# Attention in a two-layer backbone: queries split once and placed by transfers, the result norm taken for two heads at a time

## The chip, the cores and the metric

The kernel runs on one core of one Trainium2 chip. The metric is the device time of one execution in microseconds (us); of several runs the median is taken. Engines are named as the profile names them: PE is TensorE (PEld its weight loads), DVE is VectorE, ACT is ScalarE, POOL is GpSimd, SP is SyncE, which issues the kernel's transfers.

## The reference

The model has two layers over 512 latent tokens and 256 context tokens of width 1024. In each layer a norm is followed by one input projection whose columns feed three head groups: a gated MLP over positions, a differential attention, and a convolution module. An output projection joins them, and a gated FFN follows. The change touches the attention alone. It has 4 heads with two softmax maps each, queries and keys of 64 columns per map, values of 128:

```python
def diff_attn(q, k, v, lam):
    s = jnp.einsum("bqhmd,bkhmd->bhmqk", q.astype(F32), k.astype(F32)) * (B_QK_DIM ** -0.5)
    p = jax.nn.softmax(s, axis=-1)
    a = p[:, :, 0] - lam * p[:, :, 1]
    return jnp.einsum("bhqk,bkhd->bqhd", a, v.astype(F32))
...
yb = (rms_norm(o, P["subln_g"]) * (1.0 - lam_init)).astype(pa.dtype).reshape(b, n, B_WIDTH)
```

Context queries see the 256 context keys, latent queries all 768 keys. In layer 1 only latent tokens have queries. Everything is in float32.

## The kernel before

**Layout.** A product in float32 is made from rounded halves: each operand is split into a high part (type fp32r) and the remainder, and three products of the parts are added (`mm3`, lines 225 to 228). The attention products with the values, the transposes and the norms' sums are plain fp32 matmuls, which TensorE runs as two instructions each.

**Work items.** The attention stage is lines 712 to 868, once per layer. A work item n is a head h with 256 queries p: 12 items in layer 0 (first the 4 heads with context queries, which have 2 key tiles of 128, then 8 with latent queries and 6 key tiles), 8 in layer 1. Each is cut into two units of 128 queries. The loop at line 843 goes over the units: at unit u it prepares the next item's query (`q_prep`), computes the unit's two score maps, their maxima (DVE), exponentials with sums (ACT) and their difference (`scores`, `combine`); it transposes a unit two units later (`transp`), multiplies an item by its values three units later (`attn_v`), and normalizes its result five units later (`subln`).

**The query.** `q_prep` (lines 731 to 755) transposes a query into PSUM, 64 partitions for either map. The keys hold high and low parts on the two halves of the partitions, so the high part of the query of each map must stand on both halves: from the second item on one copy by ACT to `qn` and then two copies by ACT and two by POOL into `qh` place it. The low part is subtracted by DVE, 64 partitions at a time, into two standing buffers `qlz` whose other half was set to zero ahead (lines 718 to 724). Three buffers of `qh` let queries be prepared ahead of their scores; in both layers the first three are transposed at the start of the stage.

**The result norm.** The norm needs the sum of squares of 128 values plus a term with the epsilon that depends on the softmax sums (`dg`, a diagonal matrix that POOL makes per unit, line 788). `attn_v` copies the result and squares it on ACT, POOL adds `dg` (line 821), and `subln` sums over partitions by a matmul with a matrix of ones (line 828), takes logarithm and exponential on ACT, the product on DVE, and splits the result into `yBh` and `yBl`, which the output projection reads.

**Order.** Each engine runs its instructions in one fixed order. A planner sets it before the run from priorities (the order of the program, with shifts such as `SCP`) and its own estimates of durations. Beside the attention, output matmuls over the other two head groups (`wout` with part 0, lines 862 to 867) are issued into the stage as fill, on one PSUM buffer; their weights are loaded by SP and split by ACT and POOL. All transfers of the kernel are issued by SP. The launch reserves a space for descriptors of transfers issued by POOL (line 1092):

```python
_BACC = {"dynamic_dma_scratch_size": 256}
```

Of the kernel before, what the change touches and what calls it, by code (L numbers as in the profile page):

```python
# [9 lines left out]
F32 = mybir.dt.float32  # L10
F32R = mybir.dt.float32r
# [5 lines left out]
P = 128  # L17
# [9 lines left out]
QKD = 64  # L27
# [20 lines left out]
FB, WB, EB, QB = 1, 3, 5, 3  # L48
# [28 lines left out]
def tile_backbone(  # L77
# [6 lines left out]
    nc = tc.nc  # L84
    V, S, G, T = nc.vector, nc.scalar, nc.gpsimd, nc.tensor
# [19 lines left out]
    def sub_lo(o, a, hi, eng=None):  # L105
        (eng or V).tensor_sub(o, a, hi.bitcast(F32))  # L106
# [16 lines left out]
    ones = pers.tile([P, P], F32, name="ones")  # L123
# [158 lines left out]
    for l in range(DEPTH):  # L282
# [26 lines left out]
        with ExitStack() as ph:  # L309
            sac = ExitStack()  # L310
            sp = pool(sac, f"s1_{l}", side)
            ps = psum_pool(ph, f"ps1_{l}")
# [119 lines left out]
            for k2 in range(KD // 2):  # L432
                wh, wl = wsplit(wsrc(COL_C, k2), [2, 512], wengine(COL_C, k2), raw=pre.get(k2))
                for a in range(2):
                    k = 2 * k2 + a
                    for s in range(nseg)[::-1]:
                        t0, t1 = SEG[s]
                        for m in range(4):
                            ms = slice(m * P, (m + 1) * P)
                            o = pc[s][m][:, :t1 - t0]  # L440
# [3 lines left out]
                                     stop=k == KD - 1 and (s == 0 or m % 2 == 1))  # L444
# [5 lines left out]
            for s in range(nseg):  # L450
                n = SEG[s][1] - SEG[s][0]
# [19 lines left out]
            v = sp.tile([P, NT, AW], F32, name="v")  # L471
# [62 lines left out]
            sp = pool(ph, f"s1b_{l}", side)  # L534
# [47 lines left out]
            for t in range(NT_KV):  # L582
                x = kx.get(t)
                if x is None:
                    x = sp.tile([P, 512], F32, tag="kx", name="kx", bufs=KXB)
# [58 lines left out]
            for j in range(1, CONV):  # L644
                for c in range(2):
                    with low(CLOW[l]):
                        V.scalar_tensor_tensor(  # L647
                            out=cacc[:, c, :cn], in0=cin[:, c, j:j + cn], scalar=cw[:, l, c, j:j + 1],
# [5 lines left out]
            for x in range(2 * nseg):  # L654
                y = CH[l][0] + CH[l][1] * x
# [30 lines left out]
        yBh = yp.tile([P, 4, toks], F32R, name="yBh")  # L686
        yBl = yp.tile([P, 4, toks], F32R, name="yBl")
# [24 lines left out]
        with ExitStack() as ph:  # L712
            sp = pool(ph, f"s2_{l}", side)
            ps = psum_pool(ph, f"ps2_{l}")
            gsub = sp.tile([P, 1], F32, name="gsub")
            V.tensor_scalar_mul(gsub, sublt[:, l:l + 1], 1.0 - lam0)

            qlz = [sp.tile([P, 2, 256], F32R, name=f"qlz{x}") for x in range(2)]
            zero = sp.tile([P, 256], F32, name="zero")
            G.memset(zero, 0.0)  # L720
            for x in qlz:
                for m in range(2):
                    ms = slice((1 - m) * QKD, (2 - m) * QKD)
                    G.tensor_copy(x[ms, m], zero[ms])
            pairs = [(h, p) for p in range(2) for h in range(HEADS)]
            if not last:
                pairs = [(h, 2) for h in range(HEADS)] + pairs
            units = [(n, i) for n in range(len(pairs)) for i in range(2)]
            st = {}

            def q_prep(n):
                h, p = pairs[n]
                qh = sp.tile([P, 2, 256], F32R, tag="qh", name="qh", bufs=QB)
                ql = qlz[n % 2]
                pq = ps.tile([P, 256], F32, tag="w", name="pq", bufs=WB)
                for i in range(2):
                    T.transpose(pq[:, i * P:(i + 1) * P], qt[2 * p + i][:, h * P:(h + 1) * P], ident)
                if n == 0:
                    for m in range(2):
                        for a in range(2):  # L740
                            S.copy(qh[a * QKD:(a + 1) * QKD, m], pq[m * QKD:(m + 1) * QKD])
                    for m in range(2):
                        ms = slice(m * QKD, (m + 1) * QKD)
                        sub_lo(ql[ms, m], pq[ms], qh[ms, m])
                else:
                    qn = sp.tile([P, 256], F32R, tag="qn", name="qn", bufs=2)
                    S.copy(qn, pq)
                    for m in range(2):
                        src = qn[m * QKD:(m + 1) * QKD]
                        for a in range(2):  # L750
                            (G.tensor_copy if a else S.copy)(qh[a * QKD:(a + 1) * QKD, m], src)
                    for m in range(2):
                        ms = slice(m * QKD, (m + 1) * QKD)
                        sub_lo(ql[ms, m], pq[ms], qn[ms])
                st["q", n] = (qh, ql)

            def scores(n, i):
                h, p = pairs[n]
# [18 lines left out]
            def combine(n, i):  # L777
                nk = 6 if pairs[n][1] < 2 else 2
                e, sm = st[n, i]
                cc = sp.tile([P, 1], F32, tag="cc", name="cc", bufs=4)  # L780
                if i == 0:
                    st["dg", n] = sp.tile([P, 2, P], F32, tag="dg", name="dg", bufs=3)
                dg = st["dg", n][:, i]
                V.reciprocal(out=cc, in_=sm[:, 1:2])
                V.scalar_tensor_tensor(out=cc, in0=cc, scalar=nlam, in1=sm[:, 0:1], op0=ALU.mult, op1=ALU.mult)
                e0, e1 = e[0][:, :nk * P], e[1][:, :nk * P]
                V.scalar_tensor_tensor(out=e0, in0=e1, scalar=cc, in1=e0, op0=ALU.mult, op1=ALU.add)
                G.tensor_scalar(out=dg, in0=epsi, scalar1=sm[:, 0:1], scalar2=sm[:, 0:1], op0=ALU.mult, op1=ALU.mult)
                st[n, i] = e[0]

            def transp(n, i):
                nk = 6 if pairs[n][1] < 2 else 2
                e = st[n, i]
                if i == 0:
                    st[n] = sp.tile([P, 6, 256], F32, tag="ath", name="ath", bufs=2)
                at = st[n]
                for c0 in range(0, nk, 4):
                    cn_ = min(4, nk - c0)
                    pat = ps.tile([P, 4, P], F32, tag="w", name="pat", bufs=WB)
                    for c in range(cn_):  # L800
                        flip(pat[:, c], e[:, (c0 + c) * P:(c0 + c + 1) * P])
                    osl = (slice(None), slice(c0, c0 + cn_), slice(i * P, (i + 1) * P))
                    if c0 == 0:
                        S.copy(at[osl], pat[:, :cn_])
                    else:
                        V.tensor_copy(at[osl], pat[:, :cn_])

            def attn_v(n):
                h, p = pairs[n]
                k0, nk = (0, 6) if p < 2 else (LAT, 2)  # L810
                at = st[n]
                po = ps.tile([P, 256], F32, tag="w", name="po", bufs=WB)
                hs = slice(h * P, (h + 1) * P)
                for c in range(nk):
                    kt = k0 // P + c
                    T.matmul(po, vt[:, kt, hs], at[:, c], start=c == 0, stop=c == nk - 1)  # L816
                o = sp.tile([P, 256], F32, tag="o", name="o", bufs=2)
                sq = sp.tile([P, 256], F32, tag="osq", name="osq", bufs=2)
                S.copy(o, po)
                S.activation(sq, o, AF.Square)  # L820
                G.tensor_add(sq, sq, st["dg", n].rearrange("p a q -> p (a q)"))
                st["sub", n] = (o, sq)

            def subln(n):
                h, p = pairs[n]
                o, sq = st["sub", n]
                pr = ps.tile([P, 256], F32, tag="w", name="pr", bufs=WB)
                T.matmul(pr, ones, sq, start=True, stop=True)
                act(sq, pr, AF.Ln, scale=1.0 / P)
                act(sq, sq, AF.Exp, scale=-0.5)  # L830
                V.scalar_tensor_tensor(out=o, in0=o, scalar=gsub, in1=sq, op0=ALU.mult, op1=ALU.mult)
                ts = slice(p * 256, p * 256 + 256)
                S.copy(yBh[:, h, ts], o)
                sub_lo(yBl[:, h, ts], o, yBh[:, h, ts])

            first = [(g, i) for g in whole for i in range(2)]
            if l == 0:
                w0 = wout_w(0, (0,), "pool")
                g, i = first.pop(0)
                wout(0, (0,), w0, [g], ps, "f", FB, (i,))  # L840
            q_prep(0)
            nu = len(units)
            for u in range(nu + 8):
                if u < nu:
                    n, i = units[u]
                    if i == 0 and n + 1 < len(pairs):
                        with tc.high_priority(offset=SCP):
                            q_prep(n + 1)
                    with tc.high_priority(offset=SCP):
                        scores(n, i)  # L850
                    combine(n, i)
                v = u - LAG[0]
                if 0 <= v < nu:
                    transp(*units[v])
                v = u - LAG[1]
                if 0 <= v < nu and units[v][1] == 1:
                    attn_v(units[v][0])
                v = u - LAG[2]
                if 0 <= v < nu and units[v][1] == 1:
                    subln(units[v][0])  # L860

            for mp2 in range(NFILL[l]):
                if mp2 == 0 and l == 0:
# [16 lines left out]
        with ExitStack() as ph:  # L880
            pss_ = ctx.enter_context(ExitStack())
            ps = psum_pool(pss_, f"ps3_{l}")
# [9 lines left out]
            n = min(NFILL[l], NLATE[l])  # L892
# [8 lines left out]
            for x in range(len(todo) + 1):  # L901
# [3 lines left out]
                if x < len(todo):  # L905
                    mp2, w, i = todo[x]
# [208 lines left out]
```

## Time and profile before

| | |
|---|---|
| median of 3 runs | 1636.67 us (1635.95 to 1638.53) |
| profiled execution | 1637.72 us, its span 1635.9 us |
| PE busy | 1574.7 us, 96% of the span |
| DVE busy | 1033.9 us, 63% |
| ACT busy | 646.2 us, 40% |
| POOL busy | 178.3 us, 11% |
| granted TensorE clock, mean | 0.986 of full speed |
| transfers | 162.08 MB, mean 99 GB/s |

The span is what the profiler saw from the first instruction to the last; the time of the execution is a little longer. Busy time of an engine is the time with at least one instruction of it under way; matmuls overlap and their ends are modelled, so that a busy PE is not one at its peak. An engine's idle time matters only where the work that ends last waits for it. The attention stages lie at about 247 to 353 us (layer 0) and 1144 to 1228 us (layer 1) of the span.

### The profile page before, as it was taken

The numbers are of one execution on the slowest core, as the hardware profiler recorded it, in microseconds if no ns is written. First come the engines' busy times: TensorE is split into PE (matmuls) and PEld (weight loads), VectorE is DVE, ScalarE is ACT, GpSimd is POOL, SyncE is SP. The second block draws the span as 40 slices with busy tenths as digits, with TensorE's granted clock in tenths as the row PEclk, the third lists the DMA queues.
The fourth block names the chain that finished last, engine by engine and source line by source line (L and its number), as shares of the span: only waits on it lengthen the run. The fifth ranks groups of instructions, "written<-read, shape, count | busy, mean of one in ns | idle before, by whom it ended". The sixth has DMA issues, their size and how long they took to land.

```text
span 1635.9 us, 20796 instructions
## 1 busy us (share of the span) xinstructions
PE 1574.7 (96%) x8186; PEld 1294.7 (79%) x8186; DVE 1033.9 (63%) x1666; ACT 646.2 (40%) x1098; POOL 178.3 (11%) x158
## 2 busy tenths in 40 slices
PE   7999998999999999999999999779999999999999
PEld 5865776778888888888888878567778788888888
DVE  4597878969999862244333277996987544244433
ACT  5431568753523221133232244255775433123321
POOL 1130224310000000000000023341420000000000
PEclk8999999999999999999999999889999999999999
DMA  8625110014355852111122223221001223332232
GB/s 286 201 96 171 42 62 14 14 64 169 104 193 194 290 192 70 66 65 62 56 65 58 84 87 110 62 65 52 27 27 65 91 90 96 88 101 97 96 100 94
DMA packets 57409, 162.08 MB, mean 99 GB/s; under 512 B 9056, under 2 KB 11360, under 8 KB 57184
## 3 DMA queue, kind: packets, MB, share of 16 engines
q1 hardware_dynamic: 57312, 160.76, 30.3%
q8 instruction: 64, 1.05, 0.3%
q14 instruction: 33, 0.27, 0.0%
HBM read 158.64 MB, written 2.10 MB: 98 GB/s over the span
## 4 chain that ended last, share of the span: by engine, by line
PE 83%; DVE 10%; ACT 4%; issue 1%; DMA 1%; POOL 0%; POOLq 0%; DVEq 0%; SPq 0%; ACTq 0%
PE pp L227 13%; PE pp L226 13%; PE pp L228 13%; PE pd L228 6%; PE pd L226 6%; PE pd L227 6%; PE acc L389 4%; PE acc L390 4%; PE acc L397 3%; DVE cacc L647 3%; PE po L816 2%; PE mr L156 2%; PE wo L226 1%; PE wo L227 1%; PE wo L228 1%
## 5 line engine op out<-in xcount | busy, mean ns | idle before, releaser
L220 ACT CAST whi<-raw 128x1024 fp32r<-128x1024 f32 (+2 forms) x199 | 204.3, 1029 | 550.9 <-PE pp L227 251.0
L106 DVE TENSOR_TENSOR wlo<-raw,whi 128x1024 fp32r<-128x1024 f32 (+1 forms) x163 | 196.9, 1210 | 304.9 <-ACT whi L220 297.4
L227 PE MATMUL pp<-hlo,whi 128*128 128x512 f32 (+1 forms) x1072 | 380.7, 356 | 0.8 <-DVE hlo L266 0.8
L226 PE MATMUL pp<-hhi,whi 128*128 128x512 f32 (+1 forms) x1072 | 379.8, 356 | 1.5 <-ACT whi L220 1.3
L228 PE MATMUL pp<-hhi,wlo 128*128 128x512 f32 (+1 forms) x1072 | 378.9, 354 | 0.0
L226 PEld LDWEIGHTS pp<-hhi,whi 128*128 128x128 f32 x1072 | 201.4, 188 | 35.1 <-ACT whi L220 2.7
L227 PEld LDWEIGHTS pp<-hlo,whi 128*128 128x128 f32 x1072 | 201.5, 188 | 33.0 <-DVE hlo L266 1.5
L228 PEld LDWEIGHTS pp<-hhi,wlo 128*128 128x128 f32 x1072 | 201.5, 188 | 31.0
L106 POOL TENSOR_TENSOR wlo<-raw,whi 128x1024 fp32r<-128x1024 f32 (+1 forms) x36 | 100.3, 2788 | 870.3 <-ACT whi L220 716.9
L228 PE MATMUL pd<-gh,wlo 128*128 128x512 f32 (+1 forms) x550 | 192.4, 350 | 0.6 <-DVE wlo L106 0.6
L226 PE MATMUL pd<-gh,whi 128*128 128x512 f32 (+1 forms) x550 | 192.9, 351 | 0.0
L227 PE MATMUL pd<-gl,whi 128*128 128x512 f32 (+1 forms) x550 | 192.3, 350 | 0.0
L389 PE MATMUL acc<-whi,hhi 128*128 128x512 f32 x352 | 144.8, 411 | 2.8 <-ACT whi L220 2.8
L390 PE MATMUL acc<-whi,hlo 128*128 128x512 f32 x352 | 144.2, 410 | 0.0
L647 DVE SCALAR_TENSOR_TENSOR cacc<-cin,cw,cacc 128x783 f32<-128x783 f32 (+1 forms) x120 | 125.8, 1102 | 2.8 <-ACT cacc L642 2.7
L228 PEld LDWEIGHTS pd<-gh,wlo 128*128 128x128 f32 x550 | 103.4, 188 | 15.9 <-DVE wlo L106 0.8
L227 PEld LDWEIGHTS pd<-gl,whi 128*128 128x128 f32 x550 | 103.5, 188 | 15.1
L226 PEld LDWEIGHTS pd<-gh,whi 128*128 128x128 f32 x550 | 103.4, 188 | 14.9
L983 DVE TENSOR_TENSOR ft<-ft,pp 128x256 f32<-128x256 f32 (+1 forms) x66 | 39.4, 598 | 96.2 <-PE pp L228 84.7
L397 PE MATMUL acc<-wlo,hhi 128*128 128x512 f32 x352 | 94.0, 401 | 0.0
L389 PEld LDWEIGHTS acc<-whi,hhi 128*128 128x128 f32 x352 | 68.0, 193 | 25.0 <-issue 7.1
L192 DVE CUSTOM_DVE_ANT_0 mraw<-mraw,csil,bmod 128x1024 f32<-128x1024 f32 x64 | 81.7, 1280 | 8.0 <-DMA mraw<-in_w_modT_dram 7.8
(198 smaller groups left out, 2334.3 us busy)
## 6 DMA issues: line engine op xcount, KB each, us to landing
raw<-in_w_gv_dram SPq DMA_DIRECT2D x88, 512.0 KB, 3.2
mraw<-in_w_modT_dram SPq DMA_DIRECT2D x64, 512.0 KB, 4.2
raw<-in_w_in_dram SPq DMA_DIRECT2D x44, 512.0 KB, 3.6
raw<-in_w_down_dram SPq DMA_DIRECT2D x34, 512.0 KB, 3.6
mraw<-in_w_modN_dram SPq DMA_DIRECT2D x16, 512.0 KB, 5.9
mraw<-in_w_modH_dram SPq DMA_DIRECT2D x16, 512.0 KB, 3.9
raw<-in_w_out_dram SPq DMA_DIRECT2D x16, 512.0 KB, 3.2
raw<-in_w_down_dram SPq DMA_DIRECT2D x16, 384.0 KB, 3.2
```

The lines of the kernel that those rows point to most:

```text
L106: (eng or V).tensor_sub(o, a, hi.bitcast(F32))
L156: T.matmul(o[r:r + 32], cs[:, k], w, start=k < 4, stop=k >= 4, tile_position=(0, r))
L192: r = V.tensor_tensor_reduce(out=junk, in0=w, in1=csil[:, s], scale=1.0, scalar=bmod[:, l, i, f:f + 1], op0=ALU.mult, op1=ALU.add, accum_o ...
L220: S.copy(hi, raw)
L226: T.matmul(o, lhi, rhi, start=start, stop=False)
L227: T.matmul(o, lhi, rlo, start=False, stop=False)
L228: T.matmul(o, llo, rhi, start=False, stop=stop)
L389: T.matmul(pt[t], hhi[hs], wh[:, a], start=k2 + a == 0, stop=False)
L390: T.matmul(pt[t], hlo[hs], wh[:, a], start=False, stop=False)
L397: T.matmul(pt[t], hhi[hs], wl[:, a], start=False, stop=k2 + 1 == KD // 2 and a == 1)
L647: V.scalar_tensor_tensor(out=cacc[:, c, :cn], in0=cin[:, c, j:j + cn], scalar=cw[:, l, c, j:j + 1], in1=cacc[:, c, :cn], op0=ALU.mult, op1 ...
L983: V.tensor_mul(t[:, a:b], t[:, a:b], pp[s][1][:, :b - a])
```

## The change

The query is split once: one copy by ACT and one subtraction by DVE over all 128 partitions, into the two halves of a tile `qn`. Four transfers issued by POOL (`nc.gpsimd.dma_start`) then place high and low part of either map on both halves of the partitions of a tile `qq`. The zeroed buffers and the special form for the first item go. The result norm runs for two items at once, on tiles of 2 x 256 columns; the epsilon term is added by a second matmul of the ones matrix into the same PSUM tile instead of by POOL, and the `dg` tiles get 5 buffers instead of 3. Of the second part of the transposed scores (key tiles 4 and 5), the copy for the second unit of an item moves from DVE to ACT.

```diff
-            qlz = [sp.tile([P, 2, 256], F32R, name=f"qlz{x}") for x in range(2)]
-            zero = sp.tile([P, 256], F32, name="zero")
-            G.memset(zero, 0.0)
-            for x in qlz:
-                for m in range(2):
-                    ms = slice((1 - m) * QKD, (2 - m) * QKD)
-                    G.tensor_copy(x[ms, m], zero[ms])
...
             def q_prep(n):
                 h, p = pairs[n]
-                qh = sp.tile([P, 2, 256], F32R, tag="qh", name="qh", bufs=QB)
-                ql = qlz[n % 2]
+                qq = sp.tile([P, 2, 2, 256], F32R, tag="qq", name="qq", bufs=QB)
+                qn = sp.tile([P, 2, 256], F32R, tag="qn", name="qn", bufs=2)
                 pq = ps.tile([P, 256], F32, tag="w", name="pq", bufs=WB)
                 for i in range(2):
                     T.transpose(pq[:, i * P:(i + 1) * P], qt[2 * p + i][:, h * P:(h + 1) * P], ident)
-                if n == 0:
...
-                else:
-                    qn = sp.tile([P, 256], F32R, tag="qn", name="qn", bufs=2)
-                    S.copy(qn, pq)
-                    for m in range(2):
-                        src = qn[m * QKD:(m + 1) * QKD]
-                        for a in range(2):
-                            (G.tensor_copy if a else S.copy)(qh[a * QKD:(a + 1) * QKD, m], src)
-                    for m in range(2):
-                        ms = slice(m * QKD, (m + 1) * QKD)
-                        sub_lo(ql[ms, m], pq[ms], qn[ms])
-                st["q", n] = (qh, ql)
+                S.copy(qn[:, 0], pq)
+                sub_lo(qn[:, 1], pq, qn[:, 0])
+                for m in range(2):
+                    for a in range(2):
+                        nc.gpsimd.dma_start(out=qq[a * QKD:(a + 1) * QKD, :, m], in_=qn[m * QKD:(m + 1) * QKD])
+                st["q", n] = (qq[:, 0], qq[:, 1])
...
-                    st["dg", n] = sp.tile([P, 2, P], F32, tag="dg", name="dg", bufs=3)
+                    st["dg", n] = sp.tile([P, 2, P], F32, tag="dg", name="dg", bufs=5)
...
-                    if c0 == 0:
+                    if c0 == 0 or i == 1:
                         S.copy(at[osl], pat[:, :cn_])
...
-                o = sp.tile([P, 256], F32, tag="o", name="o", bufs=2)
-                sq = sp.tile([P, 256], F32, tag="osq", name="osq", bufs=2)
-                S.copy(o, po)
+                if n % 2 == 0:
+                    st["sub", n // 2] = sp.tile([P, 2, 256], F32, tag="o", name="o", bufs=2)
+                S.copy(st["sub", n // 2][:, n % 2], po)
+
+            def subln(x):
+                h, p = pairs[2 * x]
+                o = st["sub", x]
+                sq = sp.tile([P, 2, 256], F32, tag="osq", name="osq", bufs=2)
                 S.activation(sq, o, AF.Square)
-                G.tensor_add(sq, sq, st["dg", n].rearrange("p a q -> p (a q)"))
-                st["sub", n] = (o, sq)
-
-            def subln(n):
-                h, p = pairs[n]
-                o, sq = st["sub", n]
-                pr = ps.tile([P, 256], F32, tag="w", name="pr", bufs=WB)
-                T.matmul(pr, ones, sq, start=True, stop=True)
+                pr = ps.tile([P, 2, 256], F32, tag="w", name="pr", bufs=WB)
+                for y in range(2):
+                    T.matmul(pr[:, y], ones, sq[:, y], start=True, stop=False)
+                    T.matmul(pr[:, y], ones, st["dg", 2 * x + y].rearrange("p a q -> p (a q)"), start=False, stop=True)
                 act(sq, pr, AF.Ln, scale=1.0 / P)
                 act(sq, sq, AF.Exp, scale=-0.5)
                 V.scalar_tensor_tensor(out=o, in0=o, scalar=gsub, in1=sq, op0=ALU.mult, op1=ALU.mult)
-                ts = slice(p * 256, p * 256 + 256)
-                S.copy(yBh[:, h, ts], o)
-                sub_lo(yBl[:, h, ts], o, yBh[:, h, ts])
+                osl = (slice(None), slice(h, h + 2), slice(p * 256, p * 256 + 256))
+                S.copy(yBh[osl], o)
+                sub_lo(yBl[osl], o, yBh[osl])
...
-                if 0 <= v < nu and units[v][1] == 1:
-                    subln(units[v][0])
+                if 0 <= v < nu and units[v][1] == 1 and units[v][0] % 2 == 1:
+                    subln(units[v][0] // 2)
```

## Rows read from the trace of the kernel before

**Rows 1.** The page's busy table: busy us, share of the span, instructions.
```profile
PE 1574.7 (96%) x8186; PEld 1294.7 (79%) x8186; DVE 1033.9 (63%) x1666; ACT 646.2 (40%) x1098; POOL 178.3 (11%) x158
```

**Rows 2.** Windows: stretch, us, busy PE PEld DVE ACT POOL, PEclk, DMA share, GB/s.
```profile
247.00:353.00 106.00, 95.69 (x510) 77.91 (x509) 90.81 (x190) 82.38 (x217) 37.60 (x63) 0.97 0.03 11
...
267.00:343.00 76.00, 70.28 (x387) 57.69 (x387) 70.52 (x133) 60.88 (x147) 25.66 (x39) 1.00 0.03 8
...
1144.00:1228.00 84.00, 78.30 (x410) 63.05 (x409) 72.81 (x134) 62.32 (x146) 30.54 (x45) 1.00 0.08 26
...
247.00:267.00 20.00, 15.91 (x82) 12.64 (x81) 16.17 (x49) 16.81 (x58) 10.47 (x23) 0.83 0.08 27
```

**Rows 3.** TensorE in order of time: start us, us, line, out<-in, idle before it.
```profile
246.51 0.82 PE L737 MATMUL pq<-ident,q 128*128 128x128 f32 x6
...
247.72 0.39 PE L768 MATMUL pss<-kk,qh 128*128 128x256 f32 x1
...
266.93 0.45 PE L768 MATMUL pss<-kk,qh 128*128 128x512 f32 x1
...
333.10 0.40 PE L768 MATMUL pss<-kk,qh 128*128 128x512 f32 x1
...
351.32 0.70 PE L828 MATMUL pr<-osq,ones 128*128 128x256 f32 x2 [0.41 <-POOL osq L821]
...
1144.46 0.50 PE L768 MATMUL pss<-kk,qh 128*128 128x512 f32 x1
...
1207.46 0.48 PE L768 MATMUL pss<-kk,qh 128*128 128x512 f32 x1
...
1226.78 0.70 PE L828 MATMUL pr<-osq,ones 128*128 128x256 f32 x2 [0.71 <-POOL osq L821]
...
1232.80 0.40 PE L226 MATMUL wo<-yBh,whi 128*128 128x512 f32 x1
```

**Rows 4.** Groups on DVE, 267 to 345 us: count | busy us, mean ns | idle before.
```profile
L806 DVE COPY ath<-pat 128x256 f32<-128x256 f32 x15 | 6.0, 412 | 0.1
...
L106 DVE TENSOR_TENSOR qlz<-pq,qn 64x256 fp32r<-64x256 f32 x14 | 5.8, 417 | 0.1
...
L831 DVE SCALAR_TENSOR_TENSOR o<-o,gsub,osq 128x256 f32<-128x256 f32 x9 | 5.7, 632 | 0.4 <-ACT osq L97 0.3
...
L704 DVE SCALAR_TENSOR_TENSOR xT<-wo,modv,xT 128x512 f32<-128x512 f32 x2 | 1.5, 738 | 0.0
```

**Rows 5.** Groups on ScalarE (ACT), 267 to 345 us.
```profile
L751 ACT CAST qh<-qn 64x256 fp32r<-64x256 f32 x14 | 5.7, 405 | 0.2
...
L804 ACT COPY ath<-pat 128x512 f32<-128x512 f32 x15 | 8.7, 582 | 3.5 <-PE pat L109 3.3
...
L820 ACT ACTIVATE osq<-o 128x256 f32<-128x256 f32 x8 | 3.4, 422 | 0.1
```

**Rows 6.** Groups on POOL, whole span.
```profile
L788 POOL TENSOR_SCALAR dg<-epsi,sm 128x128 f32<-128x128 f32 x40 | 26.7, 666 | 60.6 <-ACT e L97 52.8 <-DVE cc L785 7.0 <-POOL qh L751 0.2
...
L821 POOL TENSOR_TENSOR osq<-osq,dg 128x256 f32<-128x256 f32 x20 | 17.5, 874 | 44.4 <-ACT osq L820 41.3 <-issue 3.1
```

**Rows 7.** The chain that ended last, near 1225 us: start, us, what.
```profile
1224.72 0.45 PE pr L828 x2
```

**Rows 8.** Transfers by line: count, KB each, median us from issue to landing.
```profile
out_dram<-xT SPq DMA_DIRECT2D x4, 128.0 KB, 1.8
...
raw<-in_w_gv_dram SPq DMA_DIRECT2D x88, 512.0 KB, 3.2
```

**Rows 9.** SP's queue in order of time, one issue that waits for nothing.
```profile
362.99 0.33 SPq L212 DMA_DIRECT2D raw<-in_w_out_dram  x1
```

**Rows 10.** POOL in order of time, ahead of the first query of either layer.
```profile
245.38 2.39 POOL L106 TENSOR_TENSOR wlo<-raw,whi 128x1024 fp32r<-128x1024 f32 x1 [2.56 <-ACT vt L677]
...
1143.55 2.38 POOL L106 TENSOR_TENSOR wlo<-raw,whi 128x1024 fp32r<-128x1024 f32 x1 [6.01 <-PE pq L737]
```

**Rows 11.** TensorE's waits, 246 to 352 us: us in total, times, longest.
```profile
PE pss L768 <- ACT e L97: 6.2, 9, 1.1
```

More of the change, by code (lines that the diff above doesn't have):

```diff
@@ L737, in q_prep @@
                     T.transpose(pq[:, i * P:(i + 1) * P], qt[2 * p + i][:, h * P:(h + 1) * P], ident)
-                if n == 0:
-                    for m in range(2):
-                        for a in range(2):
-                            S.copy(qh[a * QKD:(a + 1) * QKD, m], pq[m * QKD:(m + 1) * QKD])
-                    for m in range(2):
-                        ms = slice(m * QKD, (m + 1) * QKD)
-                        sub_lo(ql[ms, m], pq[ms], qh[ms, m])
-                else:
-                    qn = sp.tile([P, 256], F32R, tag="qn", name="qn", bufs=2)
-                    S.copy(qn, pq)
-                    for m in range(2):
-                        src = qn[m * QKD:(m + 1) * QKD]
-                        for a in range(2):
-                            (G.tensor_copy if a else S.copy)(qh[a * QKD:(a + 1) * QKD, m], src)
-                    for m in range(2):
-                        ms = slice(m * QKD, (m + 1) * QKD)
-                        sub_lo(ql[ms, m], pq[ms], qn[ms])
-                st["q", n] = (qh, ql)
+                S.copy(qn[:, 0], pq)
[4 more added lines that the diff above has]
+                st["q", n] = (qq[:, 0], qq[:, 1])
             def scores(n, i):
```

## The prediction, made before the result was known

> **What bounds the kernel now.** I read the page's busy table first, then the stretches of the two attention stages, then each engine's groups inside one of them, then TensorE's order of time, and last the transfers. The busy table says that TensorE works for 96% of the span [rows 1], so a change pays only where TensorE stands idle, or costs where it makes TensorE stand. The change lies in the two attention stages, 247 to 353 us (layer 0) and 1144 to 1228 us (layer 1). There TensorE is idle for 106.00 - 95.69 = 10.3 us and 84.00 - 78.30 = 5.7 us, together 16.0 us [rows 2]. In the steady part of layer 0, 267 to 343 us, where each head has 6 key tiles, DVE is busy 70.52 of 76 us (93%), TensorE 70.28 (92%), ScalarE 60.88 (80%) and POOL 25.66 (34%) [rows 2]: DVE and TensorE bind together, POOL has room. The first scores of a head come at 266.93 us for head 4 and 333.10 us for head 11 [rows 3], so a head takes (333.10 - 266.93) / 7 = 9.45 us; in layer 1, 1144.46 to 1207.46 us, it takes 9.0 us. From the last head's first score to the end of the last norm matmul it is 18.9 us (333.10 to 352.0) and 20.0 us (1207.46 to 1227.5) [rows 3].
>
> **DVE and ScalarE get lighter.** Per head DVE loses one of two query subtractions (0.417 us; the one that stays has 256 columns too) and one of two copies of transposed scores (0.412). The norm's product and subtraction become one each for two heads: 2 x (0.632 + 0.417) = 2.10 us go (the subtraction at the price of the query's, which has its shape's 256 columns); for their 128x512 successors the group of that shape in the same stretch gives 0.738 each, 1.48 together, so 0.31 per head [rows 4]. That is 1.14 us per head off DVE. ScalarE loses two query copies of 0.405 (0.81) and gains one score copy of 128x256, at most the 0.582 of its 128x512 copy. Its four norm passes over 128x256, some 0.42 each as the square, 1.69 a head, become four over 128x512 per pair, at 0.582 each 1.16 a head [rows 5]. It is 0.8 us per head lighter (0.81 - 0.58 + 0.53). By themselves these would let a head shrink, but only down to what TensorE needs.
>
> **TensorE gets heavier.** The epsilon term was one POOL addition per head (0.874 us) [rows 6] and becomes a second product of the ones matrix with 256 columns. The present one takes 0.45 us on the chain [rows 7], so 20 heads cost 20 x 0.45 = 9.0 us. If every idle microsecond of both stages went, the gain would be 16.0 - 9.0 = 7.0 us and no more.
>
> **The query transfers.** Before, a query went from PSUM through one ScalarE copy, then two more copies by ScalarE and two by POOL. After, it is copied (0.41 as now), subtracted (0.42), and placed by four transfers that POOL issues, each 64 partitions x 2 x 256 x 4 bytes = 128 KB. The trace has no transfer issued by POOL, so the price of one is bounded by SP's. The nearest row is the 128 KB output transfer, 1.8 us from issue to landing; weights of 512 KB take 3.2 us; an SP issue that waits for nothing holds its queue 0.33 us [rows 8, 9]. The ends: if POOL only issues and goes on, 4 x 0.33 = 1.3 us per head; if each transfer must land before the next starts, 4 x 1.8 = 7.2 to 4 x 3.2 = 12.8 us. I take them one after the other, at 1.8 + 0.33 = 2.13 us each, 8.5 us per head: the program reserves 256 bytes per partition for descriptors of such transfers (line 1092), the diff leaves that, and each of the four has 128 separate pieces of 1 KB to place.
>
> The Trainium skill speaks against the change here. Its page "DMA: Bandwidth & Descriptors", section "Anatomy of one DMA — SWDGE (gpsimd) path", gives 2.0 us + bytes / 436 GB/s for a transfer issued by GpSimd, an estimated 2.3 us for 128 KB, where SP's row shows 1.8. With 2.3 in place of 2.13 the sum below would be +61 us instead of +47.5.
>
> The Trainium skill's page "DMA: Bandwidth & Descriptors" (section "Terms") also says that a descriptor is 16 bytes and that GpSimd writes them to rings in SBUF, and (section "The descriptor swizzle") that each engine gets one more for completion on either side. By that, 256 bytes hold 16 descriptors and a transfer here needs an estimated 128 / 16 + 1 = 9, so a second one finds no room while the first is under way. No run here shows it yet.
>
> POOL also keeps two epsilon products per head, 0.666 us each [rows 6], in order with the transfers. One that waits for its exponentials stands ahead of the next query's transfers; whoever needs those is TensorE's scores, and behind them everything of that head. The subtractions of fill weights (2.4 us each [rows 10]) stand in the same queue. So POOL needs 8.5 + 1.3 = 9.85 us per head, more than the 9.45 and 9.0 of now, and more than twice the 4.8 us that each of the four context heads takes ((266.93 - 247.72) / 4) [rows 3]. Three query buffers allow a lead of two heads, which hides a latency but not a rate.
>
> **The sum.** Layer 0: the transposes start at 246.51 us [rows 3], so after 0.3 us of them, the copy and the subtraction it is ready at about 247.7; POOL is free of a weight subtraction at 247.8 [rows 10]. Query 0 has landed at 247.8 + 8.5 = 256.3, query 11 at 256.3 + 11 x 9.85 = 364.7 us, where its scores began at 333.10: 31.6 us later. Layer 1: POOL's weight subtraction holds it until 1145.9 [rows 10]; query 0 lands at 1154.4, query 7 at 1154.4 + 7 x 9.85 = 1223.4 instead of 1207.46: 15.9 us later. After the last query each stage runs on as now. The last pair's chain is longer (two more norm matmul pairs, five 128x512 passes for 128x256: about 1.6 us), which I cost at nothing, since in layer 1 output matmuls over the other head groups fill TensorE for 5.3 us (1227.5 to 1232.80) before the first that reads an attention result [rows 3]; without that cover it is 1.6 us per layer. The extra 9.0 us of TensorE and the fill matmuls lie in the waits for queries. Removing the zeroed buffers gains nothing: they stood on POOL before the first query, where the transfers stand now. Together 31.6 + 15.9 = 47.5 us. The profiled execution took 1637.72 us (span 1635.9 and 1.8 around it), which is 1.05 above the median: 1637.7 + 47.5 = 1685.2, by the median **1684 us**.
>
> By the bounds: at 1.8 us each a head costs POOL 8.53, the layers end 15.7 and 5.3 us later, total 1658; at 3.2 us, 14.1 per head, 82.9 and 50.1 later, total 1770. More TensorE idling can also lower its clock: at 247 to 267 us, with 4.1 of 20 us idle, the granted clock was 0.83 between the levels 1.2 and 2.4 GHz, against 1.00 behind it [rows 2]; that belongs to the upper part.
>
> **Rivals.** *A, faster: POOL issues and goes on.* Then it needs 1.3 + 1.3 = 2.7 us per head, the first query lands at 247.8 + 1.3 + 1.8 = 250.9, 3.2 us later than its score now, and fill matmuls cover that. DVE's 1.14 us per head come through until TensorE is full: 1637 - 7.0 = 1630 at best, some 1633 if half of it comes. For it: SP's issues of 0.33 us, and transfer engines that are nearly free (share 0.03 in layer 0) [rows 2]. Against it: the small descriptor space. It decides below about 1.9 us of POOL per transfer, where POOL falls under 9.0 us a head. Chance 0.22. *B: transfers hidden, but TensorE pays.* The idle of TensorE is mostly waits for exponentials, 6.2 us in layer 0 [rows 11], which a lighter ScalarE need not shorten, since exponentials wait for DVE's maxima. Then the 9.0 us appear, less or more what the start delays (3.2 and 4.5 us) and the relief make: 1637 + 9 = 1646, between 1637 and 1654. Chance 0.18. *My forecast, POOL's rate binds:* 0.6, own range 1656 to 1770.
>
> **Numbers.** About 0.2%, 3.3 us, can be told from no change here. Faster: 0.18 (most of A). Within: 0.10 (the rest of A, the low end of B). Slower: 0.72. The range goes from 1632, which leaves out A's best, to 1745, which leaves out the dearest transfers.
>
> **What would show it.** Right: TensorE's scores wait for the query tile's transfers, heads start some 10 us apart even with 2 key tiles, POOL's queue is occupied throughout, DVE falls well under 93% in the steady part. Wrong: first scores of head 4 near 270 us; TensorE's longest waits still on exponentials; transfers of one query that overlap. Norm matmuls must double from 40 records to 80 in any case, at 0.45 us a pair.

## The result, and the profile after

The changed kernel takes **1717.93 us** (median of 4 runs, 1715.84 to 1719.05) where the kernel before, beside it, takes 1637.32: a ratio of **1.0491** [1.0473, 1.0509], 80.6 us more. The forecast was 1684. The profiled executions differ alike: a span of 1715.8 against 1635.9 us.

The busy table of the kernel after answers [rows 1]:

```profile
PE 1601.9 (93%) x8226; PEld 1315.8 (77%) x8226; DVE 1018.2 (59%) x1610; ACT 632.6 (37%) x1032; POOL 188.7 (11%) x172
```

DVE and ScalarE have less to do, though by less than was worked out (15.7 and 13.6 us less, where 20 heads at 1.14 and 0.8 us would be 22.8 and 16). TensorE's share falls all the same, so it now stands and waits. The windows of the two attention stages, which have grown to 160 and 119 us, answer [rows 2] (same columns):

```profile
247.00:407.00 160.00, 117.78 (x572) 96.05 (x573) 83.85 (x163) 77.31 (x179) 43.58 (x73) 0.87 0.27 56
1194.00:1313.00 119.00, 92.52 (x442) 73.92 (x440) 70.17 (x111) 60.34 (x124) 31.87 (x49) 0.91 0.26 58
```

TensorE is idle for 42.2 and 26.5 us (10.3 and 5.7 before), no engine is busy for more than 78% of a stage (DVE 52% and 59%), and the granted clock fell to 0.87 and 0.91. No engine that computes is the bound. The waits of the whole span (us in total, times, longest) say what is:

```profile
POOL qq L736 <- issue: 140.9, 72, 3.9
...
PE pss L750 <- DMA qq<-qn: 57.2, 22, 4.9
```

TensorE's scores wait 57.2 us for the transferred queries; its wait for exponentials is down to 3.7. And POOL stands 140.9 us ahead of 72 of its 80 issues "for nothing that the profile shows": not for another engine, nor for data. In order of time POOL shows what this is (start us, us, line, idle before it):

```profile
247.68 0.81 POOL L736 DMA_DIRECT2D qq<-qn  x1 [0.31 <-DVE qn L106]
251.59 0.60 POOL L736 DMA_DIRECT2D qq<-qn  x1 [3.11 <-issue]
254.25 0.58 POOL L736 DMA_DIRECT2D qq<-qn  x1 [2.05 <-issue]
256.85 0.58 POOL L736 DMA_DIRECT2D qq<-qn  x1 [2.02 <-issue]
...
262.04 0.58 POOL L736 DMA_DIRECT2D qq<-qn  x1 [2.01 <-issue]
264.65 0.58 POOL L736 DMA_DIRECT2D qq<-qn  x1 [2.04 <-issue]
265.28 0.45 POOL L770 TENSOR_SCALAR dg<-epsi,sm 128x128 f32<-128x128 f32 x1
267.25 0.64 POOL L736 DMA_DIRECT2D qq<-qn  x1 [1.51 <-issue]
...
337.59 0.64 POOL L736 DMA_DIRECT2D qq<-qn  x1 [3.71 <-PE pat L109]
...
379.72 0.59 POOL L736 DMA_DIRECT2D qq<-qn  x1 [2.00 <-issue]
...
1193.39 0.66 POOL L736 DMA_DIRECT2D qq<-qn  x1
1197.92 0.59 POOL L736 DMA_DIRECT2D qq<-qn  x1 [3.87 <-issue]
...
1285.06 0.58 POOL L736 DMA_DIRECT2D qq<-qn  x1 [2.01 <-issue]
```

After the first, one transfer follows another every 2.60 us; most gaps of both stages lie between 2.56 and 2.70. An epsilon product (0.45 us at 265.28) doesn't delay the next issue: the gap around it is 2.60 too. The same query tile seen by its transfers (duration of an issue, and time to landing):

```profile
L736 POOL DMA_DIRECT2D qq<-qn x80: 578/587/811, 247.7 to 1285.1; - x80
...
DMA to landing us min/median/max: 2.3/2.3/4.2
```

A transfer lands 2.3 us after its issue (the median), and the next one is issued 0.3 us behind that. TensorE in order of time, to set against [rows 3]:

```profile
254.08 0.36 PE L750 MATMUL pss<-kk,qq 128*128 128x256 f32 x1 [2.62 <-DMA qq<-qn]
...
254.40 0.39 PE L226 MATMUL wo<-yACh,whi 128*128 128x512 f32 x1
...
259.28 0.76 PE L750 MATMUL pss<-kk,qq 128*128 128x256 f32 x2 [4.02 <-DMA qq<-qn]
...
260.26 0.63 PE L226 MATMUL wo<-yACh,whi 128*128 128x512 f32 x1
...
381.05 0.50 PE L750 MATMUL pss<-kk,qq 128*128 128x512 f32 x1 [0.33 <-ACT e L97]
...
402.05 0.59 PE L812 MATMUL pr<-dg,ones 128*128 128x256 f32 x2
403.91 0.28 PE L226 MATMUL wo<-yBh,whi 128*128 128x256 f32 x1
...
1200.39 0.77 PE L750 MATMUL pss<-kk,qq 128*128 128x512 f32 x1 [4.49 <-DMA qq<-qn]
...
1286.70 0.50 PE L750 MATMUL pss<-kk,qq 128*128 128x512 f32 x1
...
1308.60 0.59 PE L812 MATMUL pr<-dg,ones 128*128 128x256 f32 x2
1311.80 0.40 PE L226 MATMUL wo<-yBh,whi 128*128 128x512 f32 x1
```

The first output matmul that reads an attention result (L226 on yBh) marks the end of a stage. Before, in layer 0:

```profile
356.24 0.28 PE L226 MATMUL wo<-yBh,whi 128*128 128x256 f32 x1
```

It stood at 356.24 and 1232.80 us [rows 3 has the latter] and stands at 403.91 and 1311.80: 47.7 us for layer 0 and 79.0 - 47.7 = 31.3 for layer 1. The two stages account for 79.0 of the 79.9 us by which the span grew.

### The profile page after: what moved, and what is told of

It is laid out like the page before. It is cut to its first block, busy times and chain, and to the rows that moved or that the text cites. A ratio compares the mean times of both kernels' runs of the same rounds, so it can differ in the third digit from the quotient of the medians.

```text
span 1715.8 us, 20859 instructions
## 1 busy us (share of the span) xinstructions
PE 1601.9 (93%) x8226; PEld 1315.8 (77%) x8226; DVE 1018.2 (59%) x1610; ACT 632.6 (37%) x1032; POOL 188.7 (11%) x172
## 3 DMA queue, kind: packets, MB, share of 16 engines
q0 software_dynamic: 11520, 10.49, 3.4%
## 4 chain that ended last, share of the span: by engine, by line
PE 79%; DVE 8%; issue 7%; POOL 3%; ACT 3%; DMA 1%; DVEq 0%; SPq 0%; ACTq 0%; POOLq 0%
PE pp L227 12%; PE pp L226 12%; PE pp L228 12%; PE pd L228 6%; PE pd L227 6%; PE pd L226 6%; PE acc L389 3%; PE acc L390 3%; PE acc L397 3%; DVE cacc L647 3%; PE po L798 2%; POOL qq L736 2%; PE mr L156 1%; PE wo L227 1%; PE wo L228 1%
## 5 line engine op out<-in xcount | busy, mean ns | idle before, releaser
L226 PE MATMUL pp<-hhi,whi 128*128 128x512 f32 (+1 forms) x1072 | 379.8, 356 | 1.5 <-ACT whi L220 1.3
L226 PEld LDWEIGHTS pp<-hhi,whi 128*128 128x128 f32 x1072 | 201.3, 188 | 35.1 <-ACT whi L220 2.7
L226 PE MATMUL pd<-gh,whi 128*128 128x512 f32 (+1 forms) x550 | 191.8, 349 | 0.0
L750 PE MATMUL pss<-kk,qq 128*128 128x256 f32 (+1 forms) x144 | 60.5, 423 | 61.1 <-DMA qq<-qn 57.2
L753 DVE TENSOR_REDUCE mx<-pss 128x1 f32<-128x768 f32 (+1 forms) x80 | 67.6, 847 | 80.8 <-PE pss L751 80.5
L226 PEld LDWEIGHTS pd<-gh,whi 128*128 128x128 f32 x550 | 103.4, 188 | 15.1
```

The costliest lines, as they stand in the source:

```text
L226: T.matmul(o, lhi, rhi, start=start, stop=False)
L750: T.matmul(pss[:, a:b], qh[:, m, qs], kk[:, 2 * h + m, ksl], start=True, stop=False)
L753: V.tensor_reduce(out=mx, in_=pss[:, :nk * P], op=ALU.max, axis=AX.X, negate=True)
```

## The experiments

Ratios are to the kernel before on the same chip; its median there was 1638.22 us (first four kernels) and 1637.97 (the others). "After" is the changed kernel. The first theory is S, that the descriptor space lets one transfer at a time through; against it stands O, one at a time: each transfer has a price of its own on POOL, whatever the space.

The planner sets the order anew for every kernel. Compared by the traces, TensorE's order in kernels 1 and 2 is that of after, matmul for matmul. Between the other kernels compared below, some matmuls of the about 8200 stand elsewhere: 14 between 9 and 8, about 50 between 2 and 10 and between after and 3, 110 to 180 in the rest. A difference of a few us between such kernels is that of the edit together with the new order.

**1 and 2. More descriptor space.** After, with one number changed; TensorE runs the same matmuls in the same order.

```diff
-_BACC = {"dynamic_dma_scratch_size": 256}
+_BACC = {"dynamic_dma_scratch_size": 512}     # second kernel: 1024
```

> The changed kernel with 512 instead of 256 bytes of descriptor space per partition; every engine's order of instructions is the same. Theory S (space): the next transfer waits until the one before has given its descriptor space back, so twice the space lets several be under way; the distance from issue to issue inside one query falls from 2.60 us to below 1.3 us, POOL needs under 6 us per head instead of 11, TensorE's waits for the query tile fall from 57 us to under 15 us, and the time from 1718 to between 1635 and 1660 us. Theory O (one at a time): POOL's transfers follow one another whatever the space; 2.60 us stay, and 1715 to 1721 us.

> As e1, with 1024 bytes. Theory S: all four transfers of a query can be under way together; issue to issue some 0.6 us, the length of POOL's own instruction (0.587 us in the changed kernel); TensorE's second matmul of the norm then costs up to 9 us against up to 7 us of relief, so 1630 to 1650 us, a few us below or at e1. Theory O: 2.60 us and 1715 to 1721 us again.

Measured: with 512 bytes 1648.34 us, 1.0064 [1.0049, 1.0080]; with 1024 bytes 1647.03 us, 1.0052 [1.0040, 1.0065]. POOL in order of time at the start of layer 0, with 512 bytes:

```profile
247.19 1.98 POOL L736 DMA_DIRECT2D qq<-qn  x3 [0.32 <-DVE qn L106]
251.41 1.75 POOL L736 DMA_DIRECT2D qq<-qn  x3 [2.23 <-issue]
```

and with 1024 bytes:

```profile
248.30 4.29 POOL L736 DMA_DIRECT2D qq<-qn  x7 [0.31 <-DVE qn L106]
```

POOL issues 3 and then 7 transfers in a row, the 7 within 4.29 us. TensorE's waits for queries, over the whole span, with 512 and with 1024 bytes:

```profile
PE pss L750 <- DMA qq<-qn: 8.0, 6, 3.5
PE pss L750 <- DMA qq<-qn: 6.0, 3, 3.4
```

They fall from 57.2 to 8.0 and 6.0 us. One number of the launch takes 4.91% - 0.52% = 4.4% back, 72 of the 80.6 us: S is shown. A descriptor count fits the numbers 1, 3 and 7. The page's table of queues gives 11520 packets for the 80 transfers:

```profile
q0 software_dynamic: 11520, 10.49, 3.4%
```

That is 144 per transfer, 9 on each of 16 transfer engines. By the Trainium skill, page "DMA: Bandwidth & Descriptors", a descriptor has 16 bytes (section "Terms") and each engine gets one for completion on either side (section "The descriptor swizzle"), so that 256, 512 and 1024 bytes hold an estimated 16, 32 and 64 descriptors of one side, room for 1, 3 and 7 times 9. The runs agree with it: 1, 3 and 7 go at a time.

**3. Eight half transfers.** After, at 256 bytes, each transfer cut into its high and low part.

```diff
-    nc.gpsimd.dma_start(out=qq[a * QKD:(a + 1) * QKD, :, m], in_=qn[m * QKD:(m + 1) * QKD])
+    for x in range(2):
+        nc.gpsimd.dma_start(out=qq[a * QKD:(a + 1) * QKD, x, m], in_=qn[m * QKD:(m + 1) * QKD, x])
```

> The changed kernel with 256 bytes as it is, but each transfer cut into its high and its low part: eight of 64 KB per query, each with half the pieces. Theory S: two small ones fit where one fitted, so they overlap in pairs and a query takes about as long as now or less: 1690 to 1740 us. Theory O: eight times at least 2.2 us are over 17.6 us per head where 10.4 stand now, 20 heads longer by 7 us each: about 1850 us.

Measured: 1661.14 us (one run). POOL in order of time, same stretch:

```profile
251.40 1.58 POOL L737 DMA_DIRECT2D qq<-qn  x3 [2.54 <-issue]
253.59 1.70 POOL L737 DMA_DIRECT2D qq<-qn  x3 [0.60 <-issue]
```

Twice as many transfers of the same bytes, and 57 us less than after: the price is not one per transfer. S has the direction right and missed the size, since three halves fit and not two: this kernel has 12800 packets for 160 transfers, 80 each, 5 per engine, and an estimated 16 descriptors hold 3 times 5. The planner ordered some instructions of this kernel otherwise, so its 1661 is not a clean step between 1 and 2.

**4 and 6. The norm by pairs, with the old queries.** Kernel 4 is the kernel before with the norm for two heads, the epsilon product on TensorE and the moved copies; kernel 6 is kernel 4 with the epsilon added by POOL again.

```diff
 for y in range(2):
-    T.matmul(pr[:, y], ones, sq[:, y], start=True, stop=False)
-    T.matmul(pr[:, y], ones, st["dg", 2 * x + y]..., start=False, stop=True)
+    G.tensor_add(sq[:, y], sq[:, y], st["dg", 2 * x + y]...)
+T.matmul(pr..., ones, sq..., start=True, stop=True)
```

> The kernel before with the other parts of the change alone: norm for two items, epsilon by TensorE, the ScalarE copies; the queries are placed by engine copies as before. Theory P (the norm costs TensorE time): 20 more matmuls of 0.45 us are 9 us, of which the relief of DVE (0.72 us a head without the query's part) takes back some: 1638 to 1646 us. Rival N (DVE bound the stages, so its relief wins): 1630 to 1635 us.

> As e4 (norm for two items, ScalarE copies, queries by engine copies), but POOL adds the epsilon term, as before, and the ones matrix is multiplied once, 512 columns. It differs from e4 by 20 x 0.45 = 9.0 us of TensorE time. Theory P (that time is what e4 paid): 1632 to 1638 us. Rival W (the extra matmuls lay in idle time, e4 paid for the longer wait for two items): 1640 to 1643 us.

Measured: kernel 4 1641.32 us, 1.0020 [1.0011, 1.0029]; kernel 6 1637.63 us, 0.9999 [0.9991, 1.0008]. The busy tables, kernel 4:

```profile
PE 1583.2 (97%) x8226; PEld 1305.8 (80%) x8226; DVE 1025.0 (63%) x1630; ACT 645.6 (39%) x1074; POOL 160.9 (10%) x138
```

and kernel 6:

```profile
PE 1575.7 (96%) x8166; PEld 1291.8 (79%) x8166; DVE 1025.7 (63%) x1630; ACT 646.2 (40%) x1074; POOL 179.7 (11%) x158
```

Kernel 4 has 7.5 us more of TensorE's busy time than kernel 6 and is 0.21%, 3.4 us, longer. Kernel 7 below is kernel 6 without the pairs and with 3 `dg` buffers instead of 5, at 0.9981; kernel 6 is 0.18%, 2.9 us, longer. About 110 matmuls stand elsewhere in either comparison, so that pairing costs this by itself is not shown.

**5. The transferred queries alone.** The kernel before with the new `q_prep` and 1024 bytes; norm and copies as before.

```diff
+S.copy(qn[:, 0], pq)
+sub_lo(qn[:, 1], pq, qn[:, 0])
+... (the four transfers)
-_BACC = {"dynamic_dma_scratch_size": 256}
+_BACC = {"dynamic_dma_scratch_size": 1024}
```

> The kernel before with the transferred queries alone, with 1024 bytes of descriptor space. Of the 9 us by which e2 lies above the kernel before, e4 gave 3 to the norm. Theory L (latency at the start): the first query of a layer lands some 5 us later than engine copies place it, which stays as a loss while the fill covers part: 1640 to 1646 us. Rival R (relief wins): ScalarE and DVE have fewer instructions per query, so the later heads make good the start: 1634 to 1638 us.

Measured: 1639.67 us, 1.0013 [1.0004, 1.0022]: with room for descriptors the transferred queries are still no gain. The time lies between the ranges of theory L and of rival R. TensorE waits for the query tile 2.9 us in layer 0 (1.7 at the first scores, 1.2 some 15 us later) and 2.7 us in layer 1, at the first scores.

**7. The copies alone.** The kernel before, with one condition changed.

```diff
-if c0 == 0:
+if c0 == 0 or i == 1:
```

> The kernel before with only the copies of key tiles 4 and 5 for the second unit moved from DVE to ScalarE: 16 copies of 0.41 us off DVE, 0.37 us each on ScalarE. If DVE binds the steady part, 16 x 0.41 = 6.6 us come off it and some show: 1632 to 1637 us. If TensorE binds as much as DVE, no change: 1636 to 1640 us.

Measured: 1634.97 us, 0.9981 [0.9972, 0.9990], 3.1 us faster. TensorE's wait for exponentials in layer 0 falls from 6.2 us [rows 11] to 3.5, while 1.2 us of it come up in layer 1. Over the whole span it is now:

```profile
PE pss L768 <- ACT e L97: 4.7, 6, 1.2
```

That the lighter DVE made the gain, and not the new order, is not shown.

**8, 9 and 10. The start of a stage, and who adds the epsilon.** At 1024 bytes the four kernels 2, 9, 10 and 8 make a square. Kernel 9 is kernel 2 with the first query of each layer placed by engine copies instead of transfers:

```diff
+if n == 0:
+    for m in range(2):
+        for a in range(2):
+            S.copy(qq[a * QKD:(a + 1) * QKD, 0, m], pq[m * QKD:(m + 1) * QKD])
+    ... (four subtractions by DVE likewise into qq[..., 1, m])
+else:
     ... (one copy, one subtraction, four transfers)
```

Kernel 10 is kernel 2 with the epsilon added by POOL (the edit of kernel 6). Kernel 8 has both.

> All parts of the change, mended: 1024 bytes of descriptor space, the first query of each layer placed by engine copies, epsilon added by POOL. Theory: the start delay (L) and the added TensorE time (P) are the two losses left in e2, so 1647 - 6 - 6: 1632 to 1638 us. If transfers cost in another way, above 1640 us.

> e2 (1024 bytes, epsilon by TensorE) with one edit: the first query of each layer is placed by engine copies. It tells how much of e2's 9 us is the start. Theory L: the start is 6 us of it, 1640 to 1643 us. Rival: the start is covered by fill matmuls, 1645 to 1648 us.

> e2 with one other edit: POOL adds the epsilon term and the ones matrix is multiplied once (20 matmuls of 0.45 us fewer on TensorE). With e2, e8 and e9 it closes a square. Theory P: 4 to 9 us below e2, 1638 to 1643 us. Rival: the additions stand in POOL's queue behind the query transfers and hold the norm up, 1645 us or more.

| at 1024 bytes | epsilon by TensorE | epsilon by POOL |
|---|---|---|
| first query by transfers | 2: 1647.03, 1.0052 | 10: 1643.36, 1.0033 [1.0021, 1.0046] |
| first query by engines | 9: 1636.87, 0.9997 [0.9988, 1.0006] | 8: 1633.87, 0.9974 [0.9966, 0.9983] |

The start costs 0.55% and 0.59% (9.0 and 9.7 us), the epsilon on TensorE 0.19% and 0.23% (3.1 and 3.8 us). Kernel 9 lies below the range of its theory L, which put the start at 6 us, and kernel 10 just above its theory P's. Of the epsilon's two steps, that from 9 to 8 is the cleaner: the intervals don't overlap and only 14 matmuls stand elsewhere; the intervals of 2 and 10 overlap. The first scores of both layers, on TensorE in order of time, kernel 2:

```profile
252.84 0.36 PE L750 MATMUL pss<-kk,qq 128*128 128x256 f32 x1 [0.78 <-DMA qq<-qn]
...
1152.24 0.76 PE L750 MATMUL pss<-kk,qq 128*128 128x512 f32 x1 [3.42 <-DMA qq<-qn]
```

and kernel 9:

```profile
246.78 0.38 PE L759 MATMUL pss<-kk,qq 128*128 128x256 f32 x1
...
1143.33 0.50 PE L759 MATMUL pss<-kk,qq 128*128 128x512 f32 x1
```

They come 6.1 us earlier in layer 0, and 8.9 in layer 1 (with what layer 0 passes on). The end mark of layer 0 comes only 3.2 us earlier (355.55 against 358.79), that of layer 1 8.9 (1231.33 against 1240.21): in layer 0 about half of the delay was covered, in layer 1 nothing. Kernel 8 beats both the kernel before and after. Its interval overlaps that of kernel 7, which changes one condition, so that transfers or pairs add to kernel 7's gain is not shown.

**11. Two transfers instead of four.** After, at 256 bytes: only the two that cross from one half of the partitions to the other are transfers.

```diff
-for a in range(2):
-    nc.gpsimd.dma_start(out=qq[a * QKD:(a + 1) * QKD, :, m], in_=qn[m * QKD:(m + 1) * QKD])
+nc.gpsimd.dma_start(out=qq[(1 - m) * QKD:(2 - m) * QKD, :, m], in_=qn[m * QKD:(m + 1) * QKD])
+... S.copy(qq[ms, :, m], qn[ms])   # both m
```

> The changed kernel with its 256 bytes, but only the two transfers per query that cross the partition halves; ScalarE copies the other two. Theory of the rate: two transfers of 2.60 us are 5.2 us of POOL's queue per head, below the 8 to 9 us that the other engines need, so the slots cease to bind except in the context heads: 1645 to 1660 us. If the added latency and not the rate had cost the 70 us, little would come back: above 1690 us.

Measured: 1649.75 us, 1.0072 [1.0058, 1.0085]. POOL in order of time:

```profile
253.17 0.60 POOL L735 DMA_DIRECT2D qq<-qn  x1 [3.71 <-issue]
255.82 0.58 POOL L735 DMA_DIRECT2D qq<-qn  x1 [2.06 <-issue]
258.43 0.58 POOL L735 DMA_DIRECT2D qq<-qn  x1 [2.03 <-issue]
```

The transfers still go one at a time, 2.6 us apart, but a head now needs 2 x 2.6 = 5.2 us of POOL, less than the 9.0 to 9.45 us that a head takes anyway. A rate under the demand costs little beyond the start: it is 0.20% from kernel 2, which has four times its space, though also other copies and another order.

## Why the prediction was right in kind and short in size

**The bound: right.** TensorE's scores wait for the query tile, DVE falls to 52% and 59% of the stages, POOL's queue is occupied by transfers that don't overlap. Raising the descriptor space alone takes 72 us back. Layer 0 begins at 247.68 us, as forecast (247.8).

**The price of a transfer: too low.** This is the term that failed. The prediction took "1.8 + 0.33 = 2.13 us each" from SP's output transfer [rows 8, 9]. Measured are 2.3 us to landing and 2.60 from issue to issue. The last issue of layer 0 is at 379.72 us, 132.0 us and 47 gaps after the first: 11.2 us per head and not "9.85". In layer 1 it is 91.7 us for 31 gaps (1193.39 to 1285.06). Against the forecast, 48 and 32 transfers at 0.47 us more make 37.6 us. The sentence with the estimate of 2.3 us, by the Trainium skill's page "DMA: Bandwidth & Descriptors", section "Anatomy of one DMA — SWDGE (gpsimd) path", agrees with the measured landing and stood nearer than SP's row.

**The epsilon products: not a cost.** The sum put 1.3 us per head for them behind the transfers. They run while POOL would wait for the next landing, so that the 11 + 7 heads' 23.4 us were not there. This miss partly hid the one above.

**POOL's longer gaps: left out.** At 2.60 us, 47 and 31 gaps make 122.2 and 80.6 us; the stages show 132.0 and 91.7, so 9.8 + 11.1 = 20.9 us are longer gaps. Two things of about the same size make them up.

In six gaps POOL waited for another engine or worked, together 9.2 us over 2.60: it waited for the transposes ahead of 337.59, and ahead of the issue at 1230.20 stand a subtraction of fill weights (2.36 us) and three epsilon products. The prediction named this mechanism (what waits "stands ahead of the next query's transfers", and the subtractions of fill weights "stand in the same queue") and gave it no price. Waits of epsilon products for their exponentials are a small part of it: 0.43 us in layer 0 and 2.81 in layer 1 lie between transfers, the others behind the last one.

In nine gaps of more than 3.1 us the profile names nothing but "issue"; they hold 9.4 us over 2.60. There the transfer itself landed late, and in each of the nine it had company on the transfer engines. Transfers in three stretches (queue and kind: packets, MB, share; then us to landing): one of the usual gaps (259.4 to 262.0 us), the first gap of layer 0 (247.6 to 251.5), and the one from 348.86 (348.8 to 352.8):

```profile
q0 software_dynamic: 144, 0.13, 27.8%
qq<-qn POOLq DMA_DIRECT2D x1, 128.0 KB, 2.3
...
q1 hardware_dynamic: 144, 0.52, 41.7%
raw<-in_w_out_dram SPq DMA_DIRECT2D x1, 512.0 KB, 3.4
qq<-qn POOLq DMA_DIRECT2D x1, 128.0 KB, 3.6
...
q8 instruction: 1, 0.02, 2.5%
qq<-qn POOLq DMA_DIRECT2D x1, 128.0 KB, 3.7
```

The usual transfer is alone and lands after 2.3 us. The four that start at 247.68, 275.09, 337.59 and 1193.39 share the engines with a load of 512 KB of weights by SP, the five at 324.16, 348.86, 1206.02, 1240.69 and 1265.94 with one packet of the queue "instruction"; they land after 2.8 to 4.2 us. That the company is the cause is read from this coincidence; no run took it away.

Together: 37.6 - 23.4 + 20.9 = 35.1 us over the forecast 47.5, where 79.0 - 47.5 = 31.5 were measured. Of the difference 2.8 us are known: the last transfers land 2.3 and not 2.60 us after their issues (0.6), the last heads' first scores come 1.0 and 0.7 us before the landing of the fourth transfer, and the tails are 0.5 us shorter.

**The start: Rival A's ground was wrong.** It let fill matmuls cover "3.2 us" of delay. With transfers that do overlap, the start alone costs 9 to 10 us in both pairs of the square. Its issue price was low as well: an issue occupies POOL 0.59 us, not 0.33. That alone would not have decided it, since 4 x 0.59 + 1.3 is far under 9.0 us per head.

**TensorE's extra work: in part visible.** Forecast were 9.0 us that "lie in the waits for queries". Once the waits are gone, 3.1 to 3.8 us of them show, in three pairs of kernels (4 and 6, 2 and 10, 9 and 8). Rival B (1646) would thus have been close for the kernel with 1024 bytes, 1647.03, though most of that is the start and not TensorE.

**The clock: right in direction.** It is 0.87 and 0.91 in the stages against 0.97 and 1.00. At the lower of the two levels, 1.2 GHz, a fill matmul of 512 columns shows 0.63 us (at 260.26, after TensorE stood for 4.02 us; granted clock 0.50) where it shows 0.39 at the higher (at 254.40; granted clock 1.00). The window at 260 us (columns as in [rows 2]), and the busy table of kernel 2:

```profile
260.20:262.60 2.40, 2.40 (x8) 1.92 (x7) 1.14 (x4) 1.02 (x4) 0.56 (x1) 0.50 0.30 55
...
PE 1583.0 (96%) x8226; PEld 1305.2 (79%) x8226; DVE 1014.5 (62%) x1610; ACT 630.9 (38%) x1032; POOL 187.1 (11%) x172
```

TensorE's busy time grew by 27.2 us. Kernel 2 runs the same matmuls in the same order in 1583.0 us, so 18.9 of the 27.2 us went with the waits. How much of the end this added is not measured apart from the waits that caused it.

**The tail: right.** From the first score of the last head to the stage's end mark it takes 403.91 - 381.05 = 22.9 us in layer 0 and 1311.80 - 1286.70 = 25.1 in layer 1, where it took 23.1 and 25.3 before (from 333.10 and 1207.46 [rows 3]).

**The accounting.** From 1.0491 to 1.0052 is the descriptor space (72 us), to 0.9997 the start (9), to 0.9974 the epsilon on TensorE (4); what is left, the lighter engines and the new order, gains 4 us. How these 4 divide stays open: kernel 7 with the copies alone gains 3.1, the step to the pairs costs 2.9, the transferred queries with their start cost 2.1, each with an order of its own, and these single effects don't add up to the kernels that hold several of them.

## What to carry to other kernels

A transfer issued by GpSimd needs room for its descriptors while it is under way: count packets per transfer and engine against the space that the launch reserves, before moving copies to such a queue, and look for idle time "issue" at even distances ahead of its issues. In these kernels a rate too slow for the demand cost 72 us, and one fast enough little beyond the start, so that the first use in a stage can stay with the engines. One changed condition (kernel 7, 3.1 us) was worth as much here as the whole change with its three repairs (kernel 8, 4.3 us, intervals that overlap). When few us are compared, look first at whether the order of instructions stayed the same.

## What the runs showed that was not expected

- Other work of POOL runs in the wait for descriptor room: the gap between two transfers is 2.60 us with an epsilon product in it and without.
- The first transfer of each stage holds the next one back longer: 3.9 us in layer 0 and 4.5 in layer 1, against 2.60 later. Both share the transfer engines with a load of 512 KB of weights, as two later transfers do whose gaps are 3.12 and 3.35 us.
- An issue occupies POOL 0.587 us for a transfer of 128 pieces, and 0.52 us for one of 64 (kernel 3), where SP's shows 0.33 [rows 9].
- Three transfers at a time served nearly as well as seven: 1.0064 and 1.0052, intervals that overlap.
